# Holding a pair's first scores behind a set share of the projection stream, with projections handed out in half steps

## The chip, the cores and the metric

The kernel runs on one core of a Trainium2 chip. The time is device microseconds of one launch; 1162.01 us is the median of three runs of the kernel before (1161.38 to 1163.31). A lower time is better. Durations below come from one profiled execution of 1160.99 us.

## The reference

A decoder trunk of two layers, 512 tokens of width 1024 in float32. Each layer is an attention part and a squared-ReLU MLP (1024 to 4096 to 1024), each with a norm ahead and a residual around it. Layer 0 has eight heads of a dilated window mixture ("A") and eight heads of a 128-wide window with sinks on two shared key heads ("B"); layer 1 has sixteen heads of full causal attention with a forget bias ("C"). Heads are 64 wide, and q and k are normalised per head.

```python
def reference(x, ...):
    for layer in range(DEPTH):
        i = layer // 2
        h = rms_norm(x, g_mix[layer])
        if layer % 2 == 0:
            x = x + even_mixer(h, w_in_even[i], a_q_gain[i], a_k_gain[i], b_q_gain[i],
                               b_k_gain[i], b_sinks[i], w_out_even[i])
        else:
            x = x + odd_mixer(h, w_in_odd[i], b_forget[i], c_q_gain[i], c_k_gain[i], w_out_odd[i])
        h = rms_norm(x, g_mlp[layer])
        x = x + squared_relu_mlp(h, w_up[layer], w_down[layer])
    return x
...
def forgetting_attention(q, k, v, log_f):
...
        s = jnp.einsum("bqhd,bshd->bhqs", qb, k).astype(jnp.float32) * scale
        s = s + jnp.transpose(cq, (0, 2, 1))[..., None] - c_k[:, :, None, :]
        s = jnp.where((key_pos[None, :] <= t[:, None])[None, None], s, -jnp.inf)
        p = jax.nn.softmax(s, axis=-1)
        return jnp.einsum("bhqs,bshd->bqhd", p.astype(v.dtype), v)
```

## The kernel before, in words

**Products in three parts.** Every float32 product with a weight is three TensorE products: high part of the weight by high part of the activation, low by high, high by low (`project`, lines 234 to 236; `mm3`, lines 165, 168, 169, for the out-projection). A raw weight tile is loaded by SyncE (L184) into one of `RAW` = 4 buffers (tag `wraw`, which the residual tiles `xl`, L498, share); its high part `whi` is a cast (on GpSimd, L153, in the attention parts), its low part `wlo` a subtraction (L156, on VectorE or GpSimd in turn). A raw buffer is free again when its low part is made.

**Attention by pairs of heads.** A pair starts in `attend` with `get`: TensorE transposes the normalised q and k (`qkT`, L290); ScalarE and VectorE split them into high and low parts `Q` (L300, L301) and `K` (L160, L161); a DMA of SyncE copies `K` into the other half of the partitions (L313). Then come, for two heads and four blocks of 128 queries each, the scores `S` (L348, L349, and in layer 1 a mask product L351), the softmax (VectorE adds the bias and takes the maximum, L362, reading it out as `negm`; ScalarE's exponential, L365; VectorE's `rden`, L368; the scaling by it, L373, mostly on GpSimd), and one step later the values of the head before: transposes `PT` (L385), their split (L397, L398), the products `O` (L405), and `yf` (L408, L409). After a pair's second head `yf` is split into `y` (L156). Transposes, scores and `O` share four PSUM banks (pool `pB`); projections have four others (`pA`).

**The interleaving.** Each attention stage is a generator of small steps. `run` weaves it with a dense stream of other products that are ready: the projection (`pj`) for the next group of heads, or, for the last group of a layer, the out-projection (`op`, `out_part`) of the heads that are done. A dense step is handed out when its share of the stream is not ahead of the share of attention steps, moved by a lead. A projection hands out after every `GRAIN` = 4 weight and activation pairs, 12 products; `out_part` after each output block of 128 rows (12 products for four head pairs). A stage of `run` has 768 units of dense work, 144 products of 512 columns or their equivalent; the last stage of each layer counts 1536. Layer 0 has three such stages (A heads, B heads, A heads with the out-projection), layer 1 four. There are sixteen pairs in all.

**What sets the order.** What `run` traces is only the program order. A scheduler then puts each engine's instructions in its own order: those that its estimate holds ready, by priority. `tc.keep_in_program_order(m)` ties an instruction behind the one that was traced just before it on its engine; the scores have no such tie. In the final order of before, 22 to 30 dense products stand between the transposes of a pair and its first score in most pairs of the A and C heads, and 4 to 11 in the B pairs.

## Time and profile before

| | |
|---|---|
| median of three runs | 1162.01 us |
| profiled execution | 1160.99 us, its span 1159.2 us |
| TensorE matmuls busy | 1141.9 us, 99% of the span |
| VectorE, ScalarE, GpSimd busy | 873.0, 645.2, 198.1 us |
| layer 0 attention | 30 to 215 us of the span |
| MLP of layer 0 | 215 to 572 us |
| layer 1 attention | 572 to 820 us |
| MLP of layer 1 | 820 to 1159 us |

Times in the profile are microseconds from the start of the span, which is 1.8 us shorter than the profiled execution's time. In a timeline row the first number is the start, the second how long it lasted, then engine, line, operation, tile out of tiles in, how often; in brackets how long the engine had been idle before it and what released it. A busy TensorE row may overlap the next one: products of 512 columns start 0.23 us apart though each lasts 0.39 us, so two starts further apart than that are a pause. PE is TensorE, DVE VectorE, ACT ScalarE, POOL GpSimd, SPq a DMA issue of SyncE.

### The profile page before, as it was taken

The numbers are of one execution on the slowest core, as the hardware profiler recorded it, in microseconds if no ns is written. First come the engines' busy times: TensorE is split into PE (matmuls) and PEld (weight loads), VectorE is DVE, ScalarE is ACT, GpSimd is POOL, SyncE is SP. The second block draws the span as 40 slices with busy tenths as digits, with TensorE's granted clock in tenths as the row PEclk, the third lists the DMA queues.
The fourth block names the chain that finished last, engine by engine and source line by source line (L and its number), as shares of the span: only waits on it lengthen the run. The fifth ranks groups of instructions, "written<-read, shape, count | busy, mean of one in ns | idle before, by whom it ended". The sixth has DMA issues, their size and how long they took to land.

```text
span 1159.2 us, 17365 instructions
## 1 busy us (share of the span) xinstructions
PE 1141.9 (99%) x6228; PEld 977.8 (84%) x6228; DVE 873.0 (75%) x1865; ACT 645.2 (56%) x1342; POOL 198.1 (17%) x292
## 2 busy tenths in 40 slices
PE   9999999999999999999999999999999999999998
PEld 7887887888989988988988888888888888888887
DVE  7878899969868857855647877778858759669676
ACT  7555867655545455444335685655756455465452
POOL 0445434100000000000255545332100000000000
PEclk9999999999999999999999999999999999999999
DMA  8432114232333332433443433343420722523403
GB/s 288 131 91 74 55 38 146 75 108 91 93 108 92 112 105 76 123 96 111 147 128 109 110 101 98 111 129 117 161 86 18 230 80 67 188 73 111 147 34 109
DMA packets 94695, 126.57 MB, mean 109 GB/s; under 512 B 5888, under 2 KB 66304, under 8 KB 94608
## 3 DMA queue, kind: packets, MB, share of 16 engines
q1 hardware_dynamic: 93568, 123.29, 34.7%
q10 hardware_dynamic: 1040, 2.16, 0.5%
q8 instruction: 49, 0.80, 0.3%
q14 instruction: 38, 0.31, 0.1%
HBM read 114.39 MB, written 4.23 MB: 102 GB/s over the span
## 4 chain that ended last, share of the span: by engine, by line
PE 84%; DVE 8%; DMA 3%; ACT 2%; issue 2%; POOL 1%; SPq 0%; POOLq 0%; DVEq 0%; ACTq 0%
PE up L165 10%; PE up L169 10%; PE up L168 10%; PE pj L236 4%; PE pj L234 4%; PE pj L235 4%; PE O L405 3%; PE PT L385 2%; PE op L169 2%; PE op L165 2%; PE op L168 2%; PE Y L1045 2%; PE Y L1042 2%; PE Y L1044 2%; PE Y L1091 1%
## 5 line engine op out<-in xcount | busy, mean ns | idle before, releaser
L165 PE MATMUL up<-xin,whi 128*128 128x512 f32 x512 | 200.6, 392 | 0.0
L169 PE MATMUL up<-xin,whi 128*128 128x512 f32 x512 | 199.4, 389 | 0.0
L168 PE MATMUL up<-xin,wlo 128*128 128x512 f32 x512 | 199.3, 389 | 0.0
L791 ACT CAST whi<-wraw 128x512 fp32r<-128x512 f32 x228 | 139.2, 619 | 105.1 <-PE up L169 47.7
L792 DVE TENSOR_TENSOR wlo<-wraw,whi 128x512 fp32r<-128x512 f32 x228 | 151.6, 685 | 50.9 <-ACT whi L791 50.7
L169 PEld LDWEIGHTS up<-xin,whi 128*128 128x128 f32 x512 | 96.1, 188 | 20.1
L168 PEld LDWEIGHTS up<-xin,wlo 128*128 128x128 f32 x512 | 96.2, 188 | 19.9 <-issue 0.2
L165 PEld LDWEIGHTS up<-xin,whi 128*128 128x128 f32 x512 | 96.2, 188 | 19.6 <-issue 0.2
L365 ACT ACTIVATE P<-P,negm 128x128 f32<-128x128 f32 (+5 forms) x128 | 69.5, 543 | 42.7 <-DVE negm L362 40.3
L973 ACT ACTIVATE u<-up 128x512 f32<-128x512 f32 x64 | 38.3, 598 | 90.9 <-PE up L169 90.9
L234 PE MATMUL pj<-whi,hn 128*128 128x512 f32 (+2 forms) x256 | 88.7, 347 | 0.0
L236 PE MATMUL pj<-whi,hn 128*128 128x512 f32 (+2 forms) x256 | 87.0, 340 | 0.0
L235 PE MATMUL pj<-wlo,hn 128*128 128x512 f32 (+2 forms) x256 | 86.9, 339 | 0.0
L153 POOL TENSOR_SCALAR whi<-wraw 128x512 fp32r<-128x512 f32 x88 | 59.7, 680 | 158.7 <-PE pj L236 137.6
L812 DVE TENSOR_TENSOR t<-u 128x256 f32<-128x256 f32 x56 | 23.2, 423 | 62.8 <-ACT u L1116 61.1
L156 POOL TENSOR_TENSOR wlo<-wraw,whi 128x512 fp32r<-128x512 f32 x48 | 63.8, 1332 | 21.4 <-ACT whi L151 18.9
L156 DVE TENSOR_TENSOR wlo<-wraw,whi 128x512 fp32r<-128x512 f32 (+1 forms) x71 | 49.0, 698 | 18.6 <-POOL whi L153 15.1
L373 POOL TENSOR_SCALAR P<-P,rden 128x256 f32<-128x256 f32 (+2 forms) x96 | 48.0, 503 | 82.8 <-DVE rden L368 77.2
L397 ACT CAST PT<-PT 128x256 fp32r<-128x256 f32 (+3 forms) x128 | 48.9, 403 | 20.3 <-PE PT L385 19.4
L362 DVE CUSTOM_DVE_ANT_0 P<-S,bias 128x128 f32<-128x128 f32 (+1 forms) x96 | 45.7, 484 | 17.4 <-PE S L351 11.8
L791 ACT CAST whi<-mraw 128x512 fp32r<-128x512 f32 x64 | 38.8, 620 | 33.1 <-DVE mraw L902 14.4
L385 PE MATMUL PT<-ident,P 128*128 128x128 f32 x296 | 53.4, 276 | 2.4 <-DVE negm L362 1.4
(241 smaller groups left out, 3083.5 us busy)
## 6 DMA issues: line engine op xcount, KB each, us to landing
wraw<-in_w_up SPq DMA_DIRECT2D x64, 512.0 KB, 4.3
wraw<-in_w_down SPq DMA_DIRECT2D x56, 512.0 KB, 3.8
wraw<-in_w_in_odd SPq DMA_DIRECT2D x22, 512.0 KB, 3.8
wraw<-in_w_in_even SPq DMA_DIRECT2D x17, 512.0 KB, 5.0
mraw<-in_w_down SPq DMA_DIRECT2D x16, 512.0 KB, 4.7
K<-K SPq DMA_DIRECT2D x26, 256.0 KB, 2.9
bias<-csp SPq DMA_DIRECT2D x16, 256.0 KB, 3.3
wraw<-in_w_out_odd SPq DMA_DIRECT2D x8, 512.0 KB, 3.7
```

Source lines behind the costliest of these rows:

```text
L153: nc.gpsimd.tensor_scalar(dst_h, src, 1.0, 1.0, op0=OP.mult, op1=OP.mult)
L156: in_order((nc.gpsimd if lo == "pool" else nc.vector).tensor_sub(dst_l, src, dst_h.bitcast(F32)))
L165: m = nc.tensor.matmul(o, wh, xh, start=start, stop=False, skip_group_check=more)
L168: nc.tensor.matmul(o, wl, xh, start=False, stop=False, skip_group_check=more)
L169: nc.tensor.matmul(o, wh, xl, start=False, stop=stop, skip_group_check=more)
L234: nc.tensor.matmul(o, xh, hi[:, :n], start=k == 0, stop=False)
L235: nc.tensor.matmul(o, xh, lo[:, :n], start=False, stop=False)
L236: nc.tensor.matmul(o, xl, hi[:, :n], start=False, stop=k == DC - 1)
L365: nc.scalar.activation(p[:, :ne], p[:, :ne], AF.Exp, scale=-1.0, bias=negm[:, i:i + 1], accum_out=den[:, i:i + 1])
L385: nc.tensor.transpose(pt[:, (i - c) * P:(i - c + 1) * P], pr[i][:, kb * P:(kb + 1) * P], ident)
L791: sca(nc.scalar.copy(dst_h, src))
L792: late.append(lambda: vec(nc.vector.tensor_sub(dst_l, src, dst_h.bitcast(F32))))
```

## The change

After a pair's transposes `attend` now yields a number, `HOLD_K` = 0.2 (`HOLD_Q` = 0.08 for the B pairs that make no new keys). `run` takes it as a share of its dense stream and hands out dense steps until that much more has gone by, whatever the shares of the two streams are. The first score of a pair's first head is tied behind what was traced just ahead of it on TensorE. A projection now yields after every two pairs; the yields in between are of type `Half`, and `run` stops at such a half step only where the hold falls due there, so that elsewhere the grain is as before. The one place that counted steps by hand (`STATS`, at the start of layer 1) counts twice as many.

```diff
+HOLD_K = 0.2
+HOLD_Q = 0.08
...
+class Half(float):
+    pass
...
-                            if pairs % GRAIN == 0:
-                                yield GRAIN / 32 * n
+                            if pairs % 2 == 0:
+
+                                yield Half(2 / 32 * n) if pairs % GRAIN else 2 / 32 * n
...
-            def scores(q, k, j, kind, h, pr):
+            def scores(q, k, j, kind, h, pr, pin):
...
-                    nc.tensor.matmul(s[:, :n], qs, k[:, 0, k0:k0 + n], start=True, stop=False)
+                    m = nc.tensor.matmul(s[:, :n], qs, k[:, 0, k0:k0 + n], start=True, stop=False)
+                    if pin and i == 0:
+                        tc.keep_in_program_order(m)
...
-                    yield
+                    yield HOLD_K if kind != "b" or p_ == 0 else HOLD_Q
...
-                        for i, _ in enumerate(scores(q, kk[j], j, kind, h, pr)):
+                        for i, _ in enumerate(scores(q, kk[j], j, kind, h, pr, not j)):
...
-                a = d = 0
+
+                a = d = until = 0
                 while True:
-                    if d / n_dense <= (a + lead * n_att) / n_att or att is None:
+                    if d < until or d / n_dense <= (a + lead * n_att) / n_att or att is None:
                         c = next(dense, None)
+                        while isinstance(c, Half) and not d < until <= d + c:
+                            d += c
+                            c = next(dense, None)
                         if c is None:
                             break
                         d += c
                     else:
-                        if next(att, "end") == "end":
+                        share = next(att, "end")
+                        if share == "end":
                             att = None
+                        elif share:
+                            until = d + share * n_dense
                         a += 1
...
-                for _ in range(STATS):
+                for _ in range(STATS * GRAIN // 2):
```

TensorE, first pair of layer 1, the last dense products ahead of the first score and what follows (`hn` is the normalised input, the numbers tell buffers apart). Before:

```order
L234 MATMUL pj3_6732<-whi_6831,hn_6283 128x512
L235 MATMUL pj3_6732<-wlo_6832,hn_6283 128x512
L348 MATMUL S_6852<-K_6816,Q_6806 128x256
L349 MATMUL S_6852<-K_6816,Q_6806 128x256
L351 LDWEIGHTS identb_77
L351 MATMUL S_6852<-maskb_88,identb_77 128x128
```

Of the changed kernel:

```order
L240 MATMUL pj3_6732<-whi_6831,hn_6283 128x512
L241 MATMUL pj3_6732<-wlo_6832,hn_6283 128x512
L242 MATMUL pj3_6732<-whi_6831,hn_6283 128x512
L240 MATMUL pj0_6729<-whi_6861,hn_6316 128x512
L241 MATMUL pj0_6729<-wlo_6862,hn_6316 128x512
L242 MATMUL pj0_6729<-whi_6861,hn_6316 128x512
L240 MATMUL pj0_6729<-whi_6865,hn_6335 128x512
L241 MATMUL pj0_6729<-wlo_6866,hn_6335 128x512
L242 MATMUL pj0_6729<-whi_6865,hn_6335 128x512
L355 MATMUL S_6880<-K_6816,Q_6806 128x256
L358 MATMUL S_6880<-K_6816,Q_6806 128x256
```

Seven more dense products stand ahead of the first score, 30 in place of 23. Counted in the same way over the sixteen pairs, in program order, before and now: layer 0, 22 to 28, 23 to 30 (A), 7 to 10, 11 to 9, 10 or 11 to 10, 4 to 2 (B), 27 to 30, 24 to 36 (A with the out-projection); layer 1, 23 to 30, 22 or 23 to 30, 27 to 23, 24 to 24, 23 to 30, 23 to 30, and, with the out-projection, twice 23 to 36.

SyncE's queue in layer 0, around the key copies of the seventh pair (`K_2177`, `K_2181`), the first pair that runs beside the out-projection; `wraw<-in_w_out_even` are the out-projection's weights. Before:

```order
L184 DMA wraw_2235<-in_w_out_even 128x2x256 x2
L498 DMA xl_2246<-in_xt 128x2x512
L313 DMA K_1226<-K_1226 64x1024
L313 DMA K_1230<-K_1230 64x1024
L184 DMA wraw_2329<-in_w_out_even 128x2x256 x2
L498 DMA xl_2340<-in_xt 128x2x512
L184 DMA wraw_2414<-in_w_out_even 128x2x256 x2
L498 DMA xl_2425<-in_xt 128x2x512
L313 DMA K_2177<-K_2177 64x1024
L313 DMA K_2181<-K_2181 64x1024
```

Of the changed kernel:

```order
L190 DMA wraw_2186<-in_w_out_even 128x2x256 x2
L514 DMA xl_2197<-in_xt 128x2x512
L320 DMA K_1226<-K_1226 64x1024
L320 DMA K_1230<-K_1230 64x1024
L190 DMA wraw_2228<-in_w_out_even 128x2x256 x2
L514 DMA xl_2239<-in_xt 128x2x512
L320 DMA K_2177<-K_2177 64x1024
L190 DMA wraw_2414<-in_w_out_even 128x2x256
L320 DMA K_2181<-K_2181 64x1024
L190 DMA wraw_2414<-in_w_out_even 128x2x256
L514 DMA xl_2425<-in_xt 128x2x512
```

The third load of out-projection weights (`wraw_2414` in both) now stands behind the pair's first key copy, where it stood ahead of both.

VectorE at the same pair, from its first `Q` to its first softmax. Before:

```order
L301 TENSOR_TENSOR Q_2167<-qkT_2162,Q_2167 64x512
L409 TENSOR_TENSOR yf_1841<-O_2107,yf_1841 64x512
L161 SCALAR_TENSOR_TENSOR K_2177<-qkT_2172,gg_85,K_2177 64x512
L301 TENSOR_TENSOR Q_2167<-qkT_2162,Q_2167 64x512
L329 SCALAR_TENSOR_TENSOR bias_2186<-dist_100,lt_101 128x512
L161 SCALAR_TENSOR_TENSOR K_2181<-qkT_2172,gg_85,K_2181 64x512
L504 TENSOR_TENSOR acc0_0_2248<-op_2249,xl_2246 128x512
L504 TENSOR_TENSOR acc0_0_2248<-op_2283,xl_2246 128x512
L329 SCALAR_TENSOR_TENSOR bias_2300<-dist_100,lt_101 128x512
L504 TENSOR_TENSOR acc0_1_2342<-op_2343,xl_2340 128x512
L362 ISA P_2194,negm_2188<-S_2191,bias_2186 128x128
```

Of the changed kernel:

```order
L308 TENSOR_TENSOR Q_2167<-qkT_2162,Q_2167 64x512
L167 SCALAR_TENSOR_TENSOR K_2177<-qkT_2172,gg_85,K_2177 64x512
L308 TENSOR_TENSOR Q_2167<-qkT_2162,Q_2167 64x512
L162 TENSOR_TENSOR wlo_2194<-wraw_2186,whi_2193 128x512
L167 SCALAR_TENSOR_TENSOR K_2181<-qkT_2172,gg_85,K_2181 64x512
L336 SCALAR_TENSOR_TENSOR bias_2256<-dist_100,lt_101 128x512
L336 SCALAR_TENSOR_TENSOR bias_2328<-dist_100,lt_101 128x512
L520 TENSOR_TENSOR acc0_0_2199<-op_2200,xl_2197 128x512
L520 TENSOR_TENSOR acc0_0_2199<-op_2214,xl_2197 128x512
L162 TENSOR_TENSOR wlo_2418<-wraw_2414,whi_2417 128x512
L520 TENSOR_TENSOR acc0_1_2241<-op_2242,xl_2239 128x512
L371 ISA P_2264,negm_2258<-S_2261,bias_2256 128x128
```

Two low parts of out-projection weights now stand between the pair's first `Q` and its first softmax: `wlo_2194` of the first load, whose raw buffer the third load takes next, and `wlo_2418` of that third load itself. Elsewhere the counts of instructions on every engine stay as they were.

## Rows read from the trace of the kernel before

**Rows 1.** The page's busy time by engine over the span, with its share and the count of instructions.

```profile
PE 1141.9 (99%) x6228; PEld 977.8 (84%) x6228; DVE 873.0 (75%) x1865; ACT 645.2 (56%) x1342; POOL 198.1 (17%) x292
```

**Rows 2.** Busy time of each engine in two stretches, layer 0's attention and layer 1's (stretch, its length, busy time and count of PE, PEld, DVE, ACT and POOL, granted clock, DMA share, GB/s).

```profile
30.00:215.00 185.00, 176.84 (x1073) 151.44 (x1072) 159.06 (x460) 116.16 (x308) 81.55 (x137) 1.00 0.30 89
...
572.00:820.00 248.00, 246.13 (x1468) 210.78 (x1468) 186.56 (x491) 143.02 (x332) 110.94 (x141) 1.00 0.40 116
```

**Rows 3.** What TensorE waited for over the whole span (line, releaser: us in total, times, longest).

```profile
PE S L348 <- DMA K<-K: 1.7, 2, 1.2
PE PT L385 <- DVE negm L362: 1.4, 1, 1.4
PE S L348 <- DVE yf L409: 1.2, 1, 1.2
...
PE PT L385 <- POOL P L373: 0.9, 1, 0.9
```

**Rows 4.** The timeline of the first pair of layer 1, all engines.

```profile
613.17 1.04 PE L290 MATMUL qkT<-ident,qk 128*128 128x128 f32 x8
...
616.34 0.74 DVE L161 SCALAR_TENSOR_TENSOR K<-qkT,gg,K 64x512 fp32r<-64x512 f32 x1
...
617.11 2.01 SPq L313 DMA_DIRECT2D K<-K  x2
...
619.08 0.39 PE L235 MATMUL pj<-wlo,hn 128*128 128x512 f32 x1
...
620.66 0.36 PE L348 MATMUL S<-K,Q 128*128 128x256 f32 x1 [1.20 <-DMA K<-K]
```

**Rows 5.** The timeline at the first score of layer 1's second pair.

```profile
641.28 0.28 PE L235 MATMUL pj<-wlo,hn 128*128 128x256 f32 x1
641.40 0.28 PE L236 MATMUL pj<-whi,hn 128*128 128x256 f32 x1
...
642.15 0.35 PE L348 MATMUL S<-K,Q 128*128 128x256 f32 x1 [0.47 <-DMA K<-K]
```

**Rows 6.** TensorE's timeline at the first score of layer 1's seventh pair, beside the out-projection.

```profile
763.62 0.39 PE L168 MATMUL op<-y,wlo 128*128 128x512 f32 x1
764.11 0.36 PE L348 MATMUL S<-K,Q 128*128 128x256 f32 x1
```

**Rows 7.** Busy time in three shorter stretches (columns as in rows 2): the last 41 us of layer 0's attention, and the middle and the last part of layer 1's.

```profile
175.00:216.00 41.00, 39.28 (x207) 32.49 (x206) 36.19 (x82) 23.88 (x57) 15.99 (x20) 1.00 0.43 129
...
660.00:740.00 80.00, 80.00 (x494) 68.17 (x493) 59.26 (x170) 51.69 (x128) 34.96 (x48) 1.00 0.39 109
740.00:820.00 80.00, 79.79 (x470) 67.91 (x469) 66.55 (x164) 48.47 (x111) 27.63 (x36) 1.00 0.40 125
```

**Rows 8.** TensorE's timeline in layer 0, from the last B pair into the seventh pair (the first beside the out-projection).

```profile
155.21 0.40 PE L168 MATMUL op<-y,wlo 128*128 128x512 f32 x1
156.84 0.39 PE L348 MATMUL S<-K,Q 128*128 128x256 f32 x1 [1.23 <-DVE yf L409]
...
161.71 0.48 PE L168 MATMUL op<-y,wlo 128*128 128x512 f32 x1
...
167.93 0.28 PE L348 MATMUL S<-K,Q 128*128 128x256 f32 x1
...
173.04 0.38 PE L385 MATMUL PT<-ident,P 128*128 128x128 f32 x2
174.27 0.33 PE L385 MATMUL PT<-ident,P 128*128 128x128 f32 x1 [0.85 <-POOL P L373]
```

**Rows 9.** VectorE's timeline at the seventh pair.

```profile
163.46 0.73 DVE L161 SCALAR_TENSOR_TENSOR K<-qkT,gg,K 64x512 fp32r<-64x512 f32 x1
...
168.86 0.28 DVE L362 CUSTOM_DVE_ANT_0 P<-S,bias 128x128 f32<-128x128 f32 x1
...
172.49 0.69 DVE L156 TENSOR_TENSOR wlo<-wraw,whi 128x512 fp32r<-128x512 f32 x1
```

**Rows 10.** SyncE's DMA issues over the same stretch.

```profile
133.52 1.60 SPq L184 DMA_DIRECT2D wraw<-in_w_out_even  x2
...
164.22 2.74 SPq L313 DMA_DIRECT2D K<-K  x2
167.77 0.92 SPq L184 DMA_DIRECT2D wraw<-in_w_out_even  x2
```

**Rows 11.** The chain of waits of that stretch, in order of time.

```profile
168.20 4.18 DMA wraw<-in_w_out_even
172.53 1.13 POOL whi L153
```

**Rows 12.** TensorE's timeline at the eighth pair, the last of layer 0.

```profile
188.61 0.40 PE L165 MATMUL op<-y,whi 128*128 128x512 f32 x1
190.41 0.55 PE L385 MATMUL PT<-ident,P 128*128 128x128 f32 x3 [1.41 <-DVE negm L362]
```

**Rows 13.** VectorE's timeline at the eighth pair and at the end of layer 0's attention.

```profile
187.43 2.12 DVE L156 TENSOR_TENSOR wlo<-wraw,whi 128x512 fp32r<-128x512 f32 x2
...
190.08 0.27 DVE L362 CUSTOM_DVE_ANT_0 P<-S,bias 128x128 f32<-128x128 f32 x1
...
213.48 1.30 DVE L156 TENSOR_TENSOR y<-yf,y 128x512 fp32r<-128x512 f32 x1
```

**Rows 14.** GpSimd's timeline beside it.

```profile
185.88 2.52 POOL L156 TENSOR_TENSOR wlo<-wraw,whi 128x512 fp32r<-128x512 f32 x2
```

## The prediction, made before the changed kernel ran

> **What bounds the kernel now.** Read the busy time by engine first: TensorE is busy 99% of the span, VectorE, next, 75% [rows 1]. Then the same by stretch [rows 2]: layer 0's attention leaves TensorE 185.00 - 176.84 = 8.2 us idle, layer 1's 248.00 - 246.13 = 1.9 us. The change leaves the MLPs alone and takes no product away (counts on all engines stay), so about 10 us is all it could ever win, and it wins only what stood as a wait. The granted clock is 1.00, the 2.4 GHz level, in both [rows 2], so it offers nothing. Third, TensorE's waits [rows 3]: the reader is to see that few waits are at a pair's first score. Two are for the key copy (1.7 us together, layer 1), one for `yf` (1.2 us); the two largest others are at transposes `PT`, for softmax (1.4 us) and for the scaling on GpSimd (0.9 us), in layer 0.
>
> The wait that the change aims at is best seen in the first pair of layer 1 [rows 4]. The transposes start at 613.17; the path to the first score runs over ScalarE and VectorE to a key whose first half is ready at 616.34 + 0.74 = 617.1, and the copy by DMA from 617.11 lands only at 620.66, when the score starts. TensorE had 22 dense products to do in that time and began the last at 619.08. The row names 1.20 us idle; measured between starts, less the 0.23 us that a 512-column product takes, it is 620.66 - 619.08 - 0.23 = 1.35 us.
>
> **The first scores of layer 1: -2.24 us.** The same sum for the second pair is 642.15 - 641.40 - 0.12 = 0.63 us (0.12 us for a product of 256 columns, the spacing of the rows there) and for the seventh 764.11 - 763.62 - 0.23 = 0.26 us [rows 5, 6]. Together 1.35 + 0.63 + 0.26 = 2.24 us. With the hold 30 products of 0.23 us, 6.8 us, follow the transposes. In the first pair these end at 613.17 + 8 transposes to about 613.95, so the score comes at 613.95 + 6.8 = 620.75, just after the copy's landing at 620.66: the wait is covered whole, with 0.1 us to spare, and in the other two with more. What the copy's queue and the engines before it do is unchanged there. Bounds: -2.24 if all goes, 0 if the key is late by as much again; I take the first, since the path before the key holds nothing that moved.
>
> **The other first scores of layer 1: 0.** Between 660 and 740 us, with two or more pairs of 24 to 27 products ahead of the first score, TensorE is busy 80.00 of 80.00 us [rows 7]. Where the hold adds seven products to a pair that does not wait, they are missing beside its later steps, where VectorE must keep up: it is busy 59.26 of 80 us there and 66.55 of 80 in the last part [rows 7]. That is cover enough in the middle and the thinnest in the last part, where the two pairs beside the out-projection get 36 products for 23. If it fails it costs at most those 13 products, 13 x 0.23 = 3.0 us, once per pair; I take 0, as the rows of the last part have TensorE busy 79.79 of 80. Half steps add no instruction, so they cost 0; a weight is needed up to 13 products sooner, and in TensorE's list of waits no projection of the stages stands for a weight [rows 3].
>
> **Layer 0, the B pairs: 0.** Their first score has about as many products ahead as before (10 for 10). The wait of 1.23 us for `yf` at 156.84 [rows 8] is at a fourth score, which is not pinned; I leave it.
>
> **Layer 0, the seventh pair: +1.2 us.** This is where the order tells against the change. Before, the third load of out-projection weights was behind the second on SyncE, well before the pair's key copies at 164.22, and a fourth came at 167.77 [rows 10]. Now the low part of the first load (`wlo_2194`) is made on VectorE only behind the pair's first keys, so its raw buffer comes free only then, and the third load's DMA stands behind the first key copy. Two things follow.
> First, TensorE reaches the first product with `wlo_2194` ten products after the transposes: 161.71 [rows 8] + 10 x 0.23 = 164.0. VectorE has it after `K` (163.46 + 0.73 = 164.2 [rows 9]), one `Q` of 0.7 and itself 0.69 [rows 9], at about 165.5, or 0.7 earlier if its `yf` stood ahead: a wait of 0.85 to 1.5 us.
> Second, `wlo_2418` of the late load now stands on VectorE ahead of the first softmax. The load is issued at 165.5, starts to move 0.43 later and takes 4.18 us, the cast on GpSimd 1.13 [rows 11], itself 0.69: VectorE is held to about 172. The score is there at 161.71 + 30 x 0.23 + 1.2 = 169.8, so the softmax is late by 2 us; queued behind it are this pair's other softmaxes and the splits of the previous head, and four banks let TensorE run only a few scores ahead. Against it stands that before had a wait of the same kind a little later, 174.27 - 173.04 - 0.17 = 1.06 us for a `P` behind a cast of late weights [rows 8, 11], which should go as its weights come sooner. Ends: 0 if the scores and the 12 products behind them cover the late softmax and 1.06 goes; +3 if both waits stand in full (1.5 + 2.0 - 0.5). I take +1.2, near the wait for the low part alone, which has no cover at all.
>
> **Layer 0, the eighth pair: -1.2 us.** Here TensorE stands from 188.61 to 190.41, 1.58 us beyond one product, since VectorE does two low parts for 2.12 us before the first softmax at 190.08 [rows 12, 13]. With 36 products ahead of the score instead of 24 (12 x 0.23 = 2.7 us) the score comes after those low parts and the wait goes. But VectorE is busy 36.19 of the last 41 us [rows 7], and the layer ends with `y` at 213.48 + 1.30 [rows 13], which now starts from a later score: part of the gain goes into that end. Ends -1.6 and 0; I take -1.2.
>
> **Weighing a page.** Two low parts on VectorE took 2.12 us at 187.43, beside two on GpSimd from 185.88 to 188.4 [rows 13, 14], where one alone took 0.69 us [rows 9], so about 0.75 us was lost. The Trainium skill, "SBUF — State Buffer", section "SBUF: two separate sides", says that VectorE with two operands from SBUF and a GpSimd operation that reads SBUF take a shared port pair in turn, as an exclusive lock. This row agrees. By that rule `wlo_2194`, now next to two low parts of GpSimd of 1.26 us each, would come up to 1.26 us later still; the sum would be about -1.0 us, by the row alone -2.2.
>
> **The sum.** -2.24 + 0 + 1.2 - 1.2 = -2.24 us on the profiled execution's 1160.99: 1158.75. That execution is 1.02 us below the median of the runs, 1162.01; the same step from there is 1159.8.
>
> **The rivals.**
> *Layer 0 gains too.* The holds let the stream stand ahead of the scores there, and the three waits of layer 0 go without a new one: 1.2 + 0.9 + 1.4 = 3.5 us [rows 3]. For it: they all stand at VectorE or GpSimd being a little late, and layer 0 has 8.2 us of idle [rows 2]. Against it: VectorE is busy 159.06 of 185 us there [rows 2], and the seventh pair's order. 1162.01 - 2.24 - 3.5 = 1156.3.
> *Given back.* The two low parts at the seventh pair collide with GpSimd's as they did at 187.43 (1.26 us more), and the eighth pair's gain is lost in VectorE's end: -2.24 + 1.2 + 1.26 - 0.3 = -0.1, or, with the thinner cover in layer 1's last part, some tenths over: 1162.0, within 1161.0 to 1163.3. For it: VectorE's share in both last stretches, 88% and 83% [rows 7]; against it: no wait for it in layer 1 now.
> *Slower: late out-projection weights in layer 0.* The seventh pair, priced in full: 1.5 for the low part, 2.0 for the softmax held behind `wlo_2418`, and, as each later load waits for the buffer of the one before, the pairs after it start with their weights late, up to the 2.7 us by which the eighth pair's score is moved back with VectorE full behind it: 1.5 + 2.0 + 2.7 = 6.2, less 2.24 and less 0.5 of waits that go: +3.4, 1165.4. It decides once the third load lands after the pair's first score, 169.8. Against it: `op` products that need no late weight can stand in.
> *The change does not do what it says* is out for layer 1, as the order shows 30 products at its first pair; at the B pairs it is nearly so.
>
> **How the numbers follow.** Forecast 0.43 (1158.3 to 1161.0), layer 0 gains too 0.20 (1154.8 to 1158.3), given back 0.22, slower 0.15 (1163.3 to 1167). 0.2% is 2.3 us, about what a measurement here can tell from none; it puts the bounds at 1159.7 and 1164.3. Half of the forecast's cases and all of the second give 0.42 for faster; the other half, given back, and the mildest of the slower 0.45 for the same; 0.13 is left for slower. The range leaves about a tenth at each end: the lower part of layer 0's gains, the dearer part of the slower case: 1156.0 to 1163.8.
>
> **What the profile would show.** Right: no wait of a score for the key copy in layer 1's first and second pair, the score about 7 us after the transposes; in layer 0, at the seventh pair, an `op` waiting about 1 us for VectorE's low part, and no 1.4 us wait for `negm` in the eighth. Wrong: a score of layer 1 that waits still, or a `PT` of layer 1 that waits for the softmax where none did; at the seventh pair a `PT` or score that waits 2 us or more behind a late load. TensorE's idle time in the two attention stretches tells the terms apart: 8.2 and 1.9 us now, 8.2 and none by the forecast.

## The result, and the profile after

The changed kernel is slower: 1166.1 us median of six runs against 1161.77 of the kernel before, a ratio of 1.0034 (95% interval 1.0024 to 1.0044). The prediction said 1159.8 and a range up to 1163.8; both the sign and the range are missed. The profiled execution has a span of 1163.3 us, 4.1 more than before, with the granted clock at 1.00 again.

TensorE's waits over the whole span of the changed kernel, columns as in [rows 3]:

```profile
PE op L174 <- DVE wlo L162: 1.9, 1, 1.9
PE PT L394 <- DVE negm L371: 1.7, 2, 1.2
PE PT L394 <- DVE yf L418: 1.5, 1, 1.5
...
PE PT L394 <- POOL P L382: 1.1, 3, 0.6
...
PE PT L394 <- ACT P L379: 0.5, 2, 0.4
...
PE S L355 <- DMA K<-K: 0.4, 1, 0.4
```

Two things are to be seen. First scores hardly wait for a key any more (0.4 us where [rows 3] has 1.7). But transposes `PT` now wait, in more places than before, for softmax results of VectorE, GpSimd and ScalarE, and an out-projection product waits for a low part of VectorE. (The wait for `yf` is that of [rows 8], now at another instruction.)

A list of waits leaves out pauses too small for a row, so the two traces are set side by side in another way. For any two TensorE products that follow one another, take the distance of their starts less the spacing at which products of that width follow each other when nothing holds them (0.227 us for 512 columns, 0.174 for 384, 0.120 for 256, 0.066 for 128). Summed over the whole trace this is 49.3 us before and 53.4 after: the 4.1 us of the spans. By pairs, from the pair's transposes to its first score ("ahead") and from there to the next pair's transposes ("behind"), in us:

| pair | before: ahead, behind | after: ahead, behind | difference |
|---|---|---|---|
| 1, 2 (A) | 0.36, 1.93; 0.36, 1.69 | 0.36, 1.50; 0.38, 1.79 | -0.43, +0.12 |
| 3, 4 (B) | 2.78, 1.71; 0.33, 1.54 | 2.78, 1.78; 0.28, 1.12 | +0.07, -0.47 |
| 5, 6 (B) | 0.27, 1.74; 0.16, 3.06 | 0.24, 1.89; 0.17, 2.87 | +0.12, -0.18 |
| 7, 8 (A, out-projection) | 0.51, 1.94; 0.35, 4.05 | 2.65, 2.14; 0.35, 3.80 | **+2.34**, -0.25 |
| 9, 10 (C) | 1.74, 0.99; 0.97, 1.41 | 0.36, 2.24; 0.54, 2.59 | -0.13, **+0.75** |
| 11, 12 (C) | 0.35, 1.51; 0.42, 1.27 | 0.38, 1.53; 0.37, 1.28 | +0.05, -0.04 |
| 13, 14 (C) | 0.38, 1.43; 0.39, 1.59 | 0.38, 1.50; 0.36, 2.46 | +0.07, **+0.84** |
| 15, 16 (C, out-projection) | 0.62, 1.33; 0.40, 1.83 | 0.35, 2.09; 0.35, 2.58 | **+0.49**, **+0.70** |

The prediction's own gauge, TensorE's idle time in the two attention stretches (columns as in [rows 2]), reads 187.00 - 177.94 = 9.1 and 252.00 - 249.39 = 2.6 us, where it was 8.2 and 1.9 and was to become 8.2 and none:

```profile
30.00:217.00 187.00, 177.94 (x1075) 152.12 (x1075) 157.97 (x461) 115.74 (x308) 81.83 (x138) 1.00 0.30 88
574.00:826.00 252.00, 249.39 (x1470) 211.42 (x1470) 189.59 (x494) 143.82 (x335) 112.68 (x141) 1.00 0.40 117
```

By the table layer 0 loses 1.3 us, all of it at the seventh pair. Layer 1 loses 2.7: ahead of its first scores 2.2 us are gone, as forecast, and behind them 4.9 have come, in the ninth, tenth and last three pairs.

The first pair of layer 1 (the ninth) shows it. All engines' timeline of the changed kernel, which answers to [rows 4]:

```profile
614.55 1.03 PE L297 MATMUL qkT<-ident,qk 128*128 128x128 f32 x8
...
622.25 0.28 PE L355 MATMUL S<-K,Q 128*128 128x256 f32 x1
...
622.45 0.59 ACT L257 COPY qk<-pj 128x512 f32<-128x512 f32 x1 [3.26 <-PE pj L242]
...
622.97 0.08 DVE L371 DVE_READ_ACCUMULATOR2_ANT negm<- 128x1 f32 x1
...
623.07 0.63 ACT L261 ACTIVATE sq<-qk 128x512 f32<-128x512 f32 x1
623.72 1.28 ACT L374 ACT_TABLE_LOAD   x1
625.01 0.40 ACT L374 ACTIVATE P<-P,negm 128x128 f32<-128x128 f32 x1
...
626.23 0.33 PE L394 MATMUL PT<-ident,P 128*128 128x128 f32 x1 [0.61 <-POOL P L382]
```

The score comes 30 products behind the transposes and without a wait, as predicted. But seven of those products finish a projection tile earlier, so ScalarE's copy and square of that tile now stand ahead of the table load and the first exponential: `negm` is there at 623.05, the exponential starts at 625.01, and the transposes wait. Before, ScalarE's timeline had the table load over at 619.10, while the key copy was still on its way, and the exponential started with `negm`:

```profile
617.82 1.28 ACT L365 ACT_TABLE_LOAD   x1
621.58 0.40 ACT L365 ACTIVATE P<-P,negm 128x128 f32<-128x128 f32 x1 [2.47 <-DVE negm L362]
```

The seventh pair, TensorE's timeline of the changed kernel, which answers to [rows 8]:

```profile
162.39 0.39 PE L174 MATMUL op<-y,wlo 128*128 128x512 f32 x1
164.72 0.50 PE L174 MATMUL op<-y,wlo 128*128 128x512 f32 x1 [1.95 <-DVE wlo L162]
...
169.39 0.28 PE L355 MATMUL S<-K,Q 128*128 128x256 f32 x1
```

And VectorE's there, which answers to [rows 9]:

```profile
162.48 0.74 DVE L167 SCALAR_TENSOR_TENSOR K<-qkT,gg,K 64x512 fp32r<-64x512 f32 x1
163.26 0.69 DVE L308 TENSOR_TENSOR Q<-qkT,Q 64x512 fp32r<-64x512 f32 x1
163.98 0.69 DVE L162 TENSOR_TENSOR wlo<-wraw,whi 128x512 fp32r<-128x512 f32 x1
...
170.37 0.28 DVE L371 CUSTOM_DVE_ANT_0 P<-S,bias 128x128 f32<-128x128 f32 x1
```

The product waits from 162.6 for the low part that VectorE makes behind `K` and `Q`. The first softmax starts 1.0 us after its score, as it did before (168.86 after 167.93 [rows 8, 9]). At the eighth pair TensorE's timeline still has the wait of [rows 12]:

```profile
193.00 0.40 PE L171 MATMUL op<-y,whi 128*128 128x512 f32 x1
194.64 0.55 PE L394 MATMUL PT<-ident,P 128*128 128x128 f32 x3 [1.24 <-DVE negm L371]
```

### The profile page after: what moved, and what is told of

It is laid out like the page before. It is cut to its first block, busy times and chain, and to the rows that moved or that the text cites. A ratio compares the mean times of both kernels' runs of the same rounds, so it can differ in the third digit from the quotient of the medians.

```text
span 1163.3 us, 17381 instructions
## 1 busy us (share of the span) xinstructions
PE 1144.8 (98%) x6228; PEld 977.8 (84%) x6228; DVE 872.8 (75%) x1865; ACT 644.0 (55%) x1342; POOL 200.5 (17%) x292
## 4 chain that ended last, share of the span: by engine, by line
PE 86%; DVE 6%; DMA 2%; ACT 2%; POOL 2%; issue 1%; SPq 0%; POOLq 0%; ACTq 0%; DVEq 0%
PE up L171 10%; PE up L175 10%; PE up L174 10%; PE pj L240 4%; PE pj L242 4%; PE pj L241 4%; PE O L414 3%; PE PT L394 2%; PE op L175 2%; PE Y L1060 2%; PE Y L1058 2%; PE Y L1061 2%; PE op L171 2%; PE op L174 2%; PE Y L1107 1%; PE Y L1111 1%
## 5 line engine op out<-in xcount | busy, mean ns | idle before, releaser
L162 POOL TENSOR_TENSOR wlo<-wraw,whi 128x512 fp32r<-128x512 f32 x48 | 63.8, 1333 | 20.8 <-ACT whi L157 13.6
```

Source lines behind the costliest of these rows:

```text
L162: in_order((nc.gpsimd if lo == "pool" else nc.vector).tensor_sub(dst_l, src, dst_h.bitcast(F32)))
```

## The experiments

Two parts of the change could be told from the program's order alone: with the half steps but neither hold nor tie, the order on every engine is that of the kernel before, and with the holds but without the tie it is that of the changed kernel. So the holds do everything. The runs below vary where and how much is held; the tie goes with the hold. Ratios are to the kernel before, with 95% intervals.

### Each layer alone

Layer 0 alone:

```diff
-                    yield HOLD_K if kind != "b" or p_ == 0 else HOLD_Q
+                    yield None if kind == "c" else HOLD_K if kind != "b" or p_ == 0 else HOLD_Q
```

> Hold and pin in layer 0 alone (A and B pairs), layer 1 as before. Theory (each layer has its own loss): the trace of the changed kernel loses 1.3 us in layer 0, nearly all at the seventh pair, where an out-projection product waits 1.95 us for a low part on VectorE; so 1161.8 + 1.3 = 1163.1, the MLP of layer 0 starting about 1.4 us later than before and layer 1 as long as before. Rival (the loss seen in layer 1 is an echo of layer 0's later buffers and weights): near 1166, with layer 1 longer too.

Measured: 1163.15, ratio 1.0017 (1.0008 to 1.0026). The sums of pauses are 24.2 us in layer 0 (22.8 before) and 16.5 in layer 1 (16.6).

Layer 1 alone:

```diff
-                    yield HOLD_K if kind != "b" or p_ == 0 else HOLD_Q
+                    yield HOLD_K if kind == "c" else None
```

> Hold and pin in layer 1 alone (C pairs), layer 0 as before. Theory (the waits at first scores, 2.1 us, go, but 4.9 us of new pauses stand behind the first scores, since the products that were moved ahead are missing beside the softmaxes): 1161.8 + 2.7 = 1164.5. Rival (layer 1 gains by itself and only suffers from layer 0's change): 1161.8 - 2.1 = 1159.7.

Measured: 1162.84, ratio 1.0014 (1.0005 to 1.0023); pauses 22.3 us in layer 0, 18.6 in layer 1 (+2.0). The two losses, 2.1 and 1.75 us against the 1161.09 of before in that comparison, make 3.8 of the change's 4.3: each layer has its own. The rival of an echo falls.

### Layer 1: what gives the waits back

Only the ninth and tenth pair held, the two that had waited:

```diff
-                    yield HOLD_K if kind != "b" or p_ == 0 else HOLD_Q
+                    yield HOLD_K if kind == "c" and y0 == 0 else None
```

> Hold and pin only in the first two pairs of layer 1, the two whose first score waited for the key copy (1.36 and 0.63 us). Theory (given back within the same pair): the two pairs come out at -0.1 and +0.7 us, 1162.4. Rival (a hold pays where there was a wait and harms only where there was none): about -2 us, 1159.8.

Measured: 1161.99, ratio 1.0007 (0.9998 to 1.0016), which cannot be told from no change; in the trace the two pairs come out at -0.1 and +0.8 us. Where there was a wait, taking it away gained nothing.

The changed kernel with the table loaded early:

```diff
                     q, kk = get(p_)
+                    if kind == "c" and y0 + p_ == 0:
+                        tab = small.tile([P, NT], F32, tag="negm", name="tab")
+                        tc.keep_in_program_order(nc.scalar.activation(tab[:, :1], gg[:, 0:1], AF.Exp))
```

> The changed kernel, with one exponential of a 128x1 tile tied on ScalarE behind the first key of layer 1, so that the 1.28 us load of the exponential's table comes before the projection's copy and square and not behind them; it adds that one instruction and changes no result. Theory (in the first pair of layer 1 the new pause is ScalarE's: table load behind a copy and a square that the seven extra products made ready early): the two pauses at transposes there, 0.78 and 0.53 us, go, 1166.1 - 1.2 = 1164.9. Rival (the pause is for lack of dense products, whoever is late): no change, 1166.1.

Measured: 1164.63, ratio 1.0029 (1.0018 to 1.0041), that is 3.5 us slower than before where the change is 4.3. ScalarE's timeline at the ninth pair:

```profile
621.52 1.28 ACT L441 ACT_TABLE_LOAD   x1
...
625.40 0.63 ACT L261 ACTIVATE sq<-qk 128x512 f32<-128x512 f32 x1
625.94 0.39 ACT L374 ACTIVATE P<-P,negm 128x128 f32<-128x128 f32 x1
```

The exponential follows the square at once, and the pauses behind this pair's first score fall from 2.24 to 1.34 us. The intervals of the two times overlap; the 0.9 us is the trace's.

Only the ninth pair held, with the early table:

```diff
-                    yield HOLD_K if kind != "b" or p_ == 0 else HOLD_Q
+                    yield HOLD_K if kind == "c" and y0 + p_ == 0 else None
```

> Only the first pair of layer 1 is held (30 products), and the exponential's table is loaded early by one 128x1 exponential behind its first key. Everything else as before. Theory (with its key wait covered and the table load out of the way this pair keeps a gain): 1.0 us faster than before. Rival (what is moved ahead is paid back in full): no change.

Measured: 1160.95 against 1161.15, ratio 0.9999 (0.9990 to 1.0008): no change. In its trace the ninth pair gains 1.0 us and the tenth, which is not held, loses 1.0. TensorE's timeline at the tenth pair of this run:

```profile
641.22 0.36 PE L355 MATMUL S<-K,Q 128*128 128x256 f32 x1 [0.44 <-DMA K<-K]
...
643.79 0.55 PE L394 MATMUL PT<-ident,P 128*128 128x128 f32 x3 [0.80 <-DVE negm L371]
```

VectorE's timeline there:

```profile
640.87 2.14 DVE L282 TENSOR_TENSOR qk<-qk,rs 128x512 f32<-128x512 f32 x2
643.04 0.48 DVE L167 SCALAR_TENSOR_TENSOR v<-pj,rcol,v 128x256 fp32r<-128x256 f32 x1
643.45 0.28 DVE L371 CUSTOM_DVE_ANT_0 P<-S,bias 128x128 f32<-128x128 f32 x1
```

And VectorE's timeline of the kernel before, same place:

```profile
640.55 2.37 DVE L275 TENSOR_TENSOR qk<-qk,rs 128x512 f32<-128x512 f32 x2
642.95 0.48 DVE L161 SCALAR_TENSOR_TENSOR v<-pj,rcol,v 128x256 fp32r<-128x256 f32 x1
643.35 0.28 DVE L362 CUSTOM_DVE_ANT_0 P<-S,bias 128x128 f32<-128x128 f32 x1
```

The score comes 0.93 us earlier than before (642.15 [rows 5]), the softmax that reads it at 643.45 in place of 643.35. VectorE is busy without a gap up to there with the next group's normalisation and values, and TensorE merely waits at another instruction. (In the changed kernel, where the tenth pair is held too, its new pauses lie later, the largest of 0.6 us at a transpose; no run took those apart.)

Fewer held products, layer 1 alone:

```diff
-HOLD_K = 0.2
+HOLD_K = 0.166
```

> Layer 1 alone is held, by a share of 0.166 in place of 0.2, which puts 24 products ahead of each first score instead of 30 (or 36 beside the out-projection); before it was 23 in six of the eight pairs. Theory (the new pauses grow with the number of products moved ahead): the pauses behind the first scores of the second, sixth, seventh and eighth pair of layer 1 (+2 us by 30 and 36 products) nearly vanish, and the key waits of the first two come back almost whole (about 1.1 and 0.3): within 0.6 us of before. Rival (being held and placed at all costs, not how many): about 1.7 us slower, as with 30.

Measured: 1163.72, ratio 1.0025 (1.0015 to 1.0035), a miss: as bad as 30 or worse. The key waits do come back (1.1 us), but the fifteenth and sixteenth pair lose 1.35 and 1.08 us. In the fifteenth pair a weight load that landed late held VectorE at a low part, ahead of the softmax; VectorE's timeline of this run:

```profile
769.31 0.29 DVE L407 TENSOR_TENSOR PT<-PT,PT 128x128 fp32r<-128x128 f32 x1
772.74 0.69 DVE L162 TENSOR_TENSOR wlo<-wraw,whi 128x512 fp32r<-128x512 f32 x1 [3.14 <-POOL whi L159]
773.35 0.28 DVE L371 CUSTOM_DVE_ANT_0 P<-S,bias 128x128 f32<-128x128 f32 x1
```

More of them, layer 1 alone:

```diff
-HOLD_K = 0.2
+HOLD_K = 0.25
```

> Layer 1 alone is held, by a share of 0.25: 36 products ahead of the first score in seven of its eight pairs (26 in one, 23 in one, since a stage's stream ends). Theory (dose): every product past the need is missing behind the score; the four pairs that go from 30 to 36 lose some 0.5 to 1.4 us each more, 4 to 6 us slower than before in place of 1.7. Rival (the pauses are of single late instructions, such as the table load, and do not grow): about 1.7 us slower.

Measured: 1163.97, ratio 1.0027 (1.0016 to 1.0038). That is 2.9 us slower, by the medians more than with 30 (the intervals overlap), but not the 4 to 6 us of a dose; the fourteenth pair even loses less than with 30. So "products moved ahead" is no price by itself for a whole layer. In the ninth pair a pause comes only in the runs that leave few products behind the scores, and there 0.9 us of 1.3 goes with the table load. Dense products between the pair's scores and its first transposes, and the pause there:

| run | products between | pause, us |
|---|---|---|
| before | 13 | none |
| share 0.166 | 12 | none |
| share 0.2, layer 1 alone | 3 | 1.3 |
| share 0.2 and early table, that pair alone | 3 | 0.4 |
| share 0.25 | 0 | 1.5 |

Held products not counted against the stream's share, layer 1 alone:

```diff
+                free = n_dense * (1 - 2 * HOLD_K) if li else n_dense
...
-                    if d < until or d / n_dense <= (a + lead * n_att) / n_att or att is None:
+                    if d < until or (d - held) / free <= (a + lead * n_att) / n_att or att is None:
...
                             until = d + share * n_dense
+                            held += share * n_dense
```

> Layer 1 alone held (30 products, 36 at the seventh pair), but the held products are not counted against the stream's share: after a hold the rest of the projection is spread evenly over all attention steps, where the changed kernel runs attention steps without dense products until their share has caught up with the hold. In the first pair 18 products then stand among the first scores and transposes where the held kernel has none. Theory (the new pauses come from the attention steps that follow a hold without dense products between them): the pauses behind the first scores of the first two pairs fall from 4.9 to about 3 us, and layer 1 comes out near or below before: 0 to 2 us faster than before. Rival (VectorE, ScalarE and GpSimd are late whatever stands between): still about 1.7 us slower than before.

Measured: 1174.07, ratio 1.0116 (1.0102 to 1.0130), a plain miss of the theory as a remedy. With 18 products among the ninth pair's scores and transposes the pauses behind its first score are 1.01 us, as before the change (ahead of it they are 2.56, with 0.93 at a score that waits for its key once more). But the tenth, twelfth, fourteenth and fifteenth pair have 3.2 to 5.3 us each behind their first scores. In layer 1 transposes wait for `negm` (3.9 us in two) and `O` for VectorE's split (3.5 us in three). In the tenth and twelfth pair the next group's normalisation, 2.14 and 2.98 us for two products, stands on VectorE right ahead of the softmax that is waited for; and behind each of these two waits the granted clock fell to 0.50, the 1.2 GHz level, for some 3 us, which is 1.6 and 1.5 us of those two pairs' pauses. The stretch behind the first of them (columns as in [rows 2], the granted clock third from the end):

```profile
647.30:650.30 3.00, 3.00 (x14) 2.48 (x14) 2.72 (x9) 2.59 (x7) 0.92 (x2) 0.50 0.01 3
```

### Layer 1: the key's own path

Keys before q, no hold:

```diff
-                        return prep_q(qk, p_ * P), prep_k(qk, 256 + p_ * P, gg[:, 2:3])
+                        k = prep_k(qk, 256 + p_ * P, gg[:, 2:3])
+                        return prep_q(qk, p_ * P), k
```

> The kernel before without any hold, with one other edit: in layer 1 a pair's keys are split before its q, so the copy is issued about 0.7 us sooner for the first head. Theory (a first score waits for the key's chain of VectorE, ScalarE and DMA, not for want of products): the waits of 1.36 and 0.63 us shrink by up to 0.7 us each, though the scheduler now puts 20 or 21 products ahead of the score where it put 23: 0 to 1.3 us faster. Rival (the scheduler moves the score forward by as much as the key comes sooner): no change.

Measured: 1167.21, ratio 1.0050 (1.0037 to 1.0062): slower, which neither theory had. SyncE's issues at the ninth pair:

```profile
614.79 0.37 SPq L190 DMA_DIRECT2D wraw<-in_w_in_odd  x1
615.45 1.98 SPq L320 DMA_DIRECT2D K<-K  x2
```

TensorE's timeline there:

```profile
612.34 1.03 PE L297 MATMUL qkT<-ident,qk 128*128 128x128 f32 x8
...
620.10 0.36 PE L355 MATMUL S<-K,Q 128*128 128x256 f32 x1 [2.18 <-DMA K<-K]
```

The copy is issued 3.1 us behind the transposes instead of 3.9 [rows 4] and lands 7.8 behind them instead of 7.5: it now stands 0.66 us behind a weight load of 512 KB. Behind the wait the granted clock fell to half, so that of the 2.5 us that this pair loses against before 1.0 is the longer wait and 1.6 the clock:

```profile
620.70:623.70 3.00, 3.00 (x10) 2.23 (x10) 1.58 (x9) 1.80 (x6) 0.82 (x2) 0.50 0.32 116
```

The profiled execution is the fastest of five (1164.51); no trace shows what the others lost beyond it.

All low parts of the first projection stream of layer 1 on GpSimd, once with the ninth pair held and the early table, once without any hold:

```diff
-                    return project([(g * 768, g * 768 + 512)], qk_use(g, 8))
+                    return project([(g * 768, g * 768 + 512)], qk_use(g, 8), (('pool', 'pool'),) if g == 1 else PAT_ATT)
...
-                    return project([(g * 768 + 512, g * 768 + 768)], v_use(g, g))
+                    return project([(g * 768 + 512, g * 768 + 768)], v_use(g, g), (('pool', 'pool'),) if g == 1 else PAT_ATT)
```

> As the kernel with only layer 1's first pair held and the table loaded early, and besides all low parts of the first projection stream of layer 1 on GpSimd (every other pair of them was on VectorE). Two low parts of 0.69 us then leave VectorE's queue between the first pair's values and the second pair's first softmax. Theory (VectorE, with no gap in its queue from 630 us, sets when the second pair's first softmax comes, and so took back the 1 us won at the first pair): that softmax comes 0.7 to 1.4 us sooner, its wait of 0.96 us falls below 0.4, and the kernel is 0.7 to 1.2 us faster than before. Rival (the pause has another cause, or GpSimd's scaling becomes late): no change.

> The kernel before without any hold, with all low parts of the first projection stream of layer 1 on GpSimd. Theory (VectorE's queue lies on the path of the keys and of the softmaxes alike): the low part of 1.08 us ahead of the first pair's q goes, its key is copied about 1 us sooner and the key wait of 1.36 us falls to about 0.4; 0.7 to 1.5 us faster than before. Rival (the copy by DMA sets the key's time, as in the run with keys first): no change.

Measured: 1162.86, ratio 1.0013 (1.0004 to 1.0022), and 1164.87, ratio 1.0033 (1.0023 to 1.0044). Both theories missed what came. Without hold, VectorE's timeline at the ninth pair:

```profile
615.28 0.74 DVE L167 SCALAR_TENSOR_TENSOR K<-qkT,gg,K 64x512 fp32r<-64x512 f32 x1
```

And SyncE's issues there:

```profile
616.83 0.37 SPq L190 DMA_DIRECT2D wraw<-in_w_in_odd  x1
617.25 1.11 SPq L320 DMA_DIRECT2D K<-K  x2
```

The key is ready at 616.0, a microsecond earlier, as meant. But the weight load that stands ahead of it on SyncE's queue waits for a raw buffer, which GpSimd frees at 616.8, so the copy goes out at 617.25 and the score waits 2.75 us for it. The run with the hold has the same: load at 616.40, copy at 616.82, and the held score still waits 2.0 us, so the ninth pair had no gain that the tenth could have taken back. In both runs the granted clock was 0.50 for some 3 us behind this wait, and the pauses behind the ninth pair's first score are 2.6 and 2.5 us where before had 1.0. In the run with the hold the tenth pair's wait for `negm` fell from 0.96 to 0.72 us; the two low parts that were to leave VectorE's queue there still stand in it (at 632.34 and 638.23), and those that left stood ahead of the ninth pair's first softmax. That VectorE's load sets the tenth pair's softmax therefore rests on the run with the ninth pair alone; these two do not add to it.

### Layer 0: the late low part

First out-projection weights handed out at the end of the B pairs' stream:

```diff
+                def first_out():
+                    early[0] = out_weights([0, 1, 4, 5], 0)
+                    yield 0
...
-                run(att_b(), NB, chain(qk_a(1), v_a(1)), 768, LEADS[1])
+                run(att_b(), NB, chain(qk_a(1), v_a(1), first_out()), 768, LEADS[1])
-                run(chain(att_a(1), last_values()), 38, chain(out_part([0, 1, 4, 5], True),
+                run(chain(att_a(1), last_values()), 38, chain(out_part([0, 1, 4, 5], True, tiles=early),
```

> The changed kernel, with the first load of out-projection weights (two tiles, high and low parts) handed out at the end of the projection stream of the B pairs, ahead of the seventh pair's transposes; so VectorE makes the second tile's low part before that pair's q and k. Theory (the seventh pair's 2.1 us pause is that low part standing behind q and k on VectorE): the wait of an out-projection product for it goes, -1.5 to -2.1 us against the changed kernel, 4.3 us slower than before becomes 2.2 to 2.8. Rival (VectorE is simply full there, and what is made earlier delays something else by as much): no change, 4.3 us slower.

Measured: 1163.87, 2.8 us slower than before, ratio 1.0025 (1.0016 to 1.0035). The seventh pair's pauses fall from 4.8 to 3.2 us, and the wait for the low part, 2.1 of them, is gone: the low part is the cause. In its place the pair's first score waits 1.3 us for its key copy, which now goes out 1.0 us behind a load of out-projection weights.

The changed kernel without hold in the seventh and eighth pair:

```diff
-                    yield HOLD_K if kind != "b" or p_ == 0 else HOLD_Q
+                    yield None if kind == "a" and y0 == 2 else HOLD_K if kind != "b" or p_ == 0 else HOLD_Q
```

> The changed kernel without hold and pin in the last stage of layer 0 (seventh and eighth pair), so that their first scores stand where they stood. Theory: the whole loss of layer 0 sits at the seventh pair (+2.3 us) and the other six pairs gain a little (-0.9): layer 0 comes out 0.9 us shorter than before, and the kernel 1.6 to 2.1 us slower than before in place of 4.3. Rival (the loss is spread over layer 0's holds): still 3 us or more slower.

Measured: 1166.71, 5.6 us slower, ratio 1.0053 (1.0039 to 1.0067), against the theory: the wait is still there, and longer, and the granted clock fell behind it (last section). TensorE's timeline at the seventh pair:

```profile
162.57 0.39 PE L174 MATMUL op<-y,wlo 128*128 128x512 f32 x1
166.40 0.79 PE L174 MATMUL op<-y,wlo 128*128 128x512 f32 x1 [3.45 <-DVE wlo L162]
```

So it is not the seventh pair's hold that makes the low part late. The order of VectorE's instructions names another: with the hold in the B pairs alone the low part stands behind that pair's keys, with the hold in either group of A pairs alone it does not. Hence the changed kernel without holds in the B pairs:

```diff
-                    yield HOLD_K if kind != "b" or p_ == 0 else HOLD_Q
+                    yield HOLD_K if kind != "b" else None
```

> The changed kernel without hold and pin in the B pairs of layer 0 (third to sixth pair); A and C pairs held as in the change. On VectorE the low part that was late then stands where it stood before the change, 96 instructions ahead of the seventh pair's q. Theory (the hold in the B pairs pushes this low part behind the seventh pair's keys): the wait of 1.95 us for it goes and the seventh pair is as long as before the change; 1.7 to 2.3 us faster than the changed kernel, that is 2.0 to 2.6 us slower than before. Rival (the hold of the seventh pair itself does it): 4.3 us slower.

Measured: 1162.11 against 1161.19, ratio 1.0009 (1.0000 to 1.0018). The wait is gone, and the gain is larger than expected: layer 0 has 20.8 us of pauses (22.8 before), the eighth pair 1.35 less than before. The B pairs' hold was the cause of the late low part.

The A pairs' holds alone, all four and the last two:

```diff
-                    yield HOLD_K if kind != "b" or p_ == 0 else HOLD_Q
+                    yield HOLD_K if kind == "a" else None
```

> Hold and pin only in the four A pairs of layer 0; B and C pairs as before the change. Theory (the parts add up: in the run without B holds layer 0 came out 1.9 us shorter than before, mostly at the eighth pair, whose wait for a late softmax is gone, and at the first, while the C pairs lost 2.0 us): 1.9 us faster than before, 1159.3. Rival (layer 0's gain was chance of that one profile, as the first pair's pauses differ from run to run): no change, 1161.2.

```diff
-                    yield HOLD_K if kind != "b" or p_ == 0 else HOLD_Q
+                    yield HOLD_K if kind == "a" and y0 == 2 else None
```

> Hold and pin only in the seventh and eighth pair (the A pairs beside the out-projection). Theory (36 products ahead of the eighth pair's first score let VectorE finish two low parts first, and its 1.4 us wait goes, as the prediction had it): 1.2 us faster than before, 1160.0. Rival (the gain needs the holds of the first pairs too): no change.

Measured: 1159.56 against 1160.76, ratio 0.9987 (0.9978 to 0.9996), and 1160.74, ratio 0.9995 (0.9986 to 1.0003). Held in the A pairs alone the kernel is 1.2 us faster than before by the medians, 1.5 by the ratio, about 0.1%. With the last two alone the gain cannot be told from none, though the eighth pair has 1.4 us less of pauses in its trace. That pair's pauses behind its first score are not steady: 4.05 us in the trace of before, 3.5 to 3.8 in the nine runs that leave layer 0 as it was; so up to half a microsecond of such a difference is chance. In the run with all four, TensorE's timeline has there

```profile
193.99 0.33 PE L394 MATMUL PT<-ident,P 128*128 128x128 f32 x1 [0.37 <-DVE negm L371]
```

with 0.37 us in place of the 1.41 of [rows 12].

## Why the prediction was wrong

**The first scores of layer 1 (-2.24).** The waits went, 2.2 us, as worked out. What failed is the step that booked them as a gain, together with the next step, **the other first scores, 0**. It priced a hold only where a pair had not waited, and took the absence of softmax waits in the kernel before as cover. But VectorE and ScalarE needed that time: at the tenth pair, with the ninth alone held, the softmax comes at the same time although its score comes 0.93 us sooner. Behind the first scores 4.9 us came back; the price of 0 should have been about +4.9 for layer 1 (net +2.7; +2.0 with layer 1 held alone). In the ninth pair ScalarE's table load of 1.28 us, which had been over before the key landed, came out behind a copy and a square: a cover taken away that the working never named. The prediction had written down the sign of this: a `PT` of layer 1 that waits for the softmax where none did. Of the 4.9 us the ninth and tenth pair, the two that had waited, took 2.4; the fourteenth to sixteenth took 2.4 more, and there the cause is not shown (below).

**The seventh pair (+1.2).** The mechanism was right: `wlo` behind `K` and `Q`, seen in the order. Its first half, 0.85 to 1.5 us, measured 1.95 idle: the low part came at 164.7, somewhat sooner than reckoned (165.5), but TensorE arrived at 162.6 and not at 164.0. The second half, a first softmax held 2 us by the late load, did not come: that load landed in time for its cast at 168.50, and the softmax started 1.0 us after its score. The pair lost 2.3 in all. The cause was given to the wrong hold: it lies in the B pairs, and their step, priced at **0**, cost these 2 us from a distance.

**The eighth pair (-1.2).** In the changed kernel -0.25: with 36 products ahead of the first score the transposes still wait 1.24 us for `negm`, so the hold alone does not take the wait away. With the same hold and no hold in the B pairs the three traces have -0.9 to -1.4. It is tempting to say that the late low part ate the gain, but two runs speak against it: with the low part handed out early and all holds in place a wait of 0.8 us for `negm` stays and the pair gains 0.2, and in the run without hold at this pair, with the low part late, the pair gains 0.8 all the same. What decides this wait stays open.

**Steps that were not priced.** The first two A pairs have no step in the sum; they measured -0.43 and +0.12, and the B pairs, at 0, measured -0.5 together. One reading was loose without touching the sum: [rows 3] was read as showing the wait for `yf` at a first score, and the prediction itself puts it at a fourth one further down.

**The rivals.** "Slower" named 1165.4, near the result, but that is in good part luck: of the 6.2 us that it set on layer 0's weights 2.3 were there, and the rest of the loss came in layer 1, where it still counted a gain of 2.24. "Given back" had the right kind of mechanism, VectorE as the bound, and was argued down with "no wait for it in layer 1 now". That is the misreading to remember: in [rows 3] TensorE waits for the key, so VectorE's lateness has no row.

**The page that was weighed.** The rule of the Trainium skill ("SBUF — State Buffer", section "SBUF: two separate sides") did not come to bear here: the late low part took 0.69 us, as GpSimd had finished its two low parts by 161.9.

What stays open is why the pairs that had hardly waited (fourteenth to sixteenth; the fifteenth 0.26 us) lose 0.5 to 0.8 us each in the changed kernel, together 2.0 of its 4.1. With layer 1 held alone they lose 0.2 to 0.8 each with 30 or 36 products ahead, and up to 1.35 with 24, one product more than before. Their pauses lie at `O`, at transposes and at scores behind late softmaxes, one of them behind a late weight; no single run separated these.

## What to carry to other kernels

A wait on the bound engine that goes is a gain only if the engines behind it would be ready sooner too: compare, in absolute time, when the next consumer's input is made, not only which wait ends last. Before filling a wait with other work, list what the other engines do under it (a table load, a normalisation, a low part) and what the moved work triggers on them. In a kernel whose order a scheduler makes, a change in one stage can move a low-priority instruction a stage later; it is cheapest found by taking the change away stage by stage in the order, before anything runs.

## What the hardware showed that was not expected

TensorE's granted clock fell to half, the 1.2 GHz level, for about 3 us in six of the sixteen profiles of the experiments (eight times in all, the last microseconds of the span left out), each time right behind pauses of TensorE: twice with the early table, twice with the held products not counted, and once each with keys first, in the two runs with low parts on GpSimd and in the run without hold in the seventh and eighth pair. In the kernel before and the changed kernel it did not. The seven times within the attention stretches cost 1.5 to 1.8 us each. With the early table one fall came after three short pauses, while the third pair's transposes waited for the normalised q and k; the busy times of that stretch (columns as in [rows 2], the granted clock third from the end):

```profile
103.90:107.00 3.10, 3.10 (x8) 2.52 (x9) 0.92 (x2) 1.16 (x2) 1.74 (x2) 0.50 0.01 3
```

In the run without hold in the seventh pair it fell after that pair's pause of 3.45 us:

```profile
166.30:169.30 3.00, 2.90 (x10) 2.61 (x11) 1.10 (x5) 0.35 (x2) 0.00 (x0) 0.50 0.80 199
```

In the first stretch products of 512 columns start 0.43 us apart in place of 0.23, some 1.5 us lost. The changed kernel has the same three pauses at that place and shows a clock of 1.00 behind them:

```profile
103.30:106.30 3.00, 3.00 (x18) 2.47 (x16) 2.08 (x4) 1.08 (x2) 1.52 (x3) 1.00 0.00 0
```

Its pause of 2.1 us at the seventh pair was not followed by a fall either, while pauses of 2.0 and 2.2 us with the held products not counted were. So a pause can cost more than its length, in some executions and not in others, and the losses of the runs above with long waits are in part this.

How soon the key's copy lands goes with how close it follows a 512 KB load on SyncE. From issue to the score that waits for it: 3.55 us when issued 1.49 us after the load [rows 4, with the load at 615.62], 4.65 us at 0.66 us, 5.1 us at 0.42 us. The run with the hold and low parts on GpSimd has 5.8 us at 0.42 us. Over all traces here the 22 first copies of a pair that were issued within 0.8 us behind such a load landed 4.2 to 5.6 us after their issue, the 36 issued 1.0 to 1.8 us behind a load 3.1 to 4.7, and the 126 issued 1.8 to 9 us behind one 2.8 to 3.5. In these runs making a key earlier did not bring it sooner after the transposes.
